# Output weights 6 and 7 and the first projection operand ordered behind the last attention blocks

## The chip, the cores and the metric

The kernel runs on one core of a Trainium2 chip. The metric is the device time of one execution in microseconds (us); lower is better. A core has five engines with a queue each: TensorE (PE, matrix products; PEld is its weight load), VectorE (DVE), ScalarE (ACT), GpSimd (POOL) and SyncE (SP, which here only issues transfers). Each engine takes its instructions in the order that was fixed when the program was built, and an instruction that waits holds up everything behind it on its engine.

## What is computed

The reference is an encoder of two layers on 1024 tokens of width 1024, in float32:

```python
for i in range(2):
    mix = mla_mixer(h, ...) if i == 0 else diff_mixer(h, ...)
    h = layernorm(ALPHA * h + mix)
    h = layernorm(ALPHA * h + swiglu(h))
```

The change lies in layer 0, where the mixer ends and its output projection begins. The mixer is an attention of 8 heads; a token sees the keys of its own chunk of 64 tokens and of all chunks before. With `o` the eight heads' results side by side (8 x 128 = 1024 columns), the mixer returns `o @ w_o`, and the layer goes on with `layernorm(ALPHA * x + o @ w_o)`.

## The kernel before, in words

**Precision by parts.** Products run on a float32 form that TensorE reads in one pass but that keeps fewer bits. So an operand is split in two: ACT casts it to that form (`hi`), and DVE or POOL subtracts (`lo = x - hi`). A product is then three matmuls, hi x hi, hi x lo and lo x hi (`mm3`, L140).

**Attention of layer 0.** Work goes by (head, block of 128 queries). For each block `score_a` (L1141) and `softmax_block` (L206) make the scores on PE (L216), add the mask and find the maximum on DVE (L219), take the exponential on ACT (L222) and the reciprocal of its sum on DVE (L224), and scale the row by it on POOL (L1150). Then `transpose_block` (L227) transposes the block's probabilities on PE (L148), and for each pair of transposed squares ACT makes the hi part `pth` (L243) and DVE the lo part `ptl` (L244). For each pair of blocks, `pv_group` (L246) multiplies with the values on PE (L255), ACT copies the result to `ob` (L1160), and SP stores it to the scratch `o_dr` in memory (L1161). `attention` (L258) runs the blocks of a head in rising order, but those of the last head, 7, in `LAST_ORDER` = 6, 7, 4, 5, 2, 3, 0, 1. Scores run two blocks ahead. The last block of all is therefore block 1 of head 7.

**Output projection.** `out_proj` (L278) loads the eight heads' output weights (128 x 1024 each) and splits them: `load_w` (L128) issues the load on SP (L132), casts on ACT (L136) and subtracts on POOL (L137). Weight 6 goes to a tile of its own pool, and weight 7 to one of the kernel's large tiles; both raw copies lie in the tag `wr`, which has two buffers and is also used by the first loads of the feed-forward part (`gp`, L541). Then, for the token blocks 6, 7, 4, 5, ..., it loads the block's `o` of all heads (`of`, L299; it needs `o_dr` written for head 7), casts it on ACT (`oh`, L302), subtracts on DVE (L303; the profile shows that tile as `oh_a` too), and multiplies: 24 matmuls for each half of the output's columns (three for each head, heads in rising order), into `zp`. DVE adds the residual (L314), and a layer norm follows. The trace calls the first halves' matmuls `zp_a` on L143 to L145.

**What sets the order.** The code is traced as written, and a planner then fixes each engine's order from priorities and from its own model of how long things take. It may put a cast of `out_proj` ahead of attention work that stands earlier in the text, if its model has the cast ready first. `behind(i, j)` (L155) adds an order without a semaphore between two instructions of one engine: `i` stands behind `j` in that engine's queue.

Of the kernel before, what the change touches and what calls it, by code (L numbers as in the profile page):

```python
# [9 lines left out]
F32 = mybir.dt.float32  # L10
F32R = mybir.dt.float32r
AF = mybir.ActivationFunctionType
ALU = mybir.AluOpType
# [3 lines left out]
P = 128  # L17
# [4 lines left out]
H = 8  # L22
# [16 lines left out]
LAST_ORDER = (6, 7, 4, 5, 2, 3, 0, 1)  # L39
# [3 lines left out]
def trunk(  # L43
# [32 lines left out]
    nc = tc.nc  # L76
    V, A, G, T = nc.vector, nc.scalar, nc.gpsimd, nc.tensor
# [9 lines left out]
    wp = ctx.enter_context(tc.tile_pool(name="wp", bufs=3))  # L87
# [19 lines left out]
    def f32(t):  # L107
        return t.bitcast(F32)

    def big_tile(name, dt=F32R):  # L110
        return big.tile([P, 2, 1024], dt, tag="big", name=name)

    def ps_s(name):
        return ps.tile([P, 512], F32, tag="s", bufs=ps_bufs[0], name=name)
# [4 lines left out]
    def ps_t(name):  # L119
        return ps.tile([P, 512], F32, tag="t", bufs=ps_bufs[2], name=name)  # L120
# [4 lines left out]
    def small(name, n=1):  # L125
        return sp.tile([P, 2], F32, tag="small", name=name, bufs=22)[:, :n]

    def load_w(src, cols, name, hi=None, lo=None, eng=None, raw=None, ins=False):  # L128

        if raw is None:  # L130
            raw = wp.tile([P, 1024], F32, tag="wr", bufs=2, name=f"r_{name}")
        nc.sync.dma_start(raw[:, :cols], src)  # L132
        if hi is None:
            hi = wp.tile([P, 1024], F32R, tag="wh", name=f"h_{name}")
            lo = wp.tile([P, 1024], F32R, tag="wl", name=f"l_{name}")
        A.copy(hi[:, :cols], raw[:, :cols])  # L136
        j = (eng or G).tensor_tensor(lo[:, :cols], raw[:, :cols], f32(hi[:, :cols]), ALU.subtract)  # L137
        return (hi, j.ins) if ins else (hi, lo)

    def mm3(ps_out, pairs):  # L140
        n = len(pairs)
        for i, (lh, ll, rh, rl) in enumerate(pairs):
            T.matmul(ps_out, lh, rh, start=(i == 0), stop=False)  # L143
            T.matmul(ps_out, lh, rl, start=False, stop=False)  # L144
            T.matmul(ps_out, ll, rh, start=False, stop=(i == n - 1))  # L145

    def tr(ps_out, in_):
        T.transpose(ps_out, in_, ident)  # L148

    def bcast_row(pool, src, n, name, tag):  # L150
        t = pool.tile([P, n], F32, tag=tag, name=name, bufs=1)
        nc.gpsimd.dma_start(t, src.partition_broadcast(P))
        return t

    def behind(i, j):  # L155

        tc.add_manual_dep(
            i, j.name,
            mybir.DependencyInfo(mybir.DependencyClass.NoSync, mybir.DependencyReason.DATA),
            reason="kept in program order",  # L160
        )
# [37 lines left out]
    def new_xT(pool, name):  # L199
# [3 lines left out]
        }  # L203
        return [[t[p, hf] for hf in range(2)] for p in range(2)]

    def softmax_block(lp, q_pass, s_bias, i, scale, name):  # L206
        n = (i + 1) * P
        nb = 1 if n <= 512 else 2
        w = n // nb
        l = lp.tile([P, 1024], F32, tag="l", name=f"l_{name}")  # L210
        mx = BIGF
        for b in range(nb):
            s = ps_s(f"s_{name}_{b}")
            ks = slice(b * w, (b + 1) * w)
            for j, (lh, rh) in enumerate(q_pass):
                T.matmul(s[:, :w], lh, rh[:, ks], start=(j == 0), stop=(j == len(q_pass) - 1))  # L216
            bv = s_bias[:, 896 - P * i + b * w:896 - P * i + (b + 1) * w]
            m = small(f"mx_{name}_{b}")
            V.tensor_tensor_reduce(l[:, ks], s[:, :w], bv, -scale, mx, ALU.add, ALU.min, m)  # L219
            mx = m  # L220
        sm = small(f"sm_{name}")
        A.activation(l[:, :n], l[:, :n], AF.Exp, bias=mx, scale=-1.0, accum_out=sm)  # L222
        r = small(f"r_{name}")
        V.reciprocal(r, sm)  # L224
        return l, r

    def transpose_block(ptp, pts, l, i, name):  # L227
        qc = (i % 2) * P
        for jq in range(i // 4 + 1):
            nj = min(4, i + 1 - 4 * jq)  # L230
            pt = ps_t(f"pt_{name}_{jq}")
            for jj in range(nj):
                j = 4 * jq + jj
                tr(pt[:, jj * P:(jj + 1) * P], l[:, j * P:(j + 1) * P])
            for jp in range(2 * jq, 2 * jq + (nj + 1) // 2):
                n = min(2, i + 1 - 2 * jp)
                if i % 2 == 0:
                    pts[jp] = tuple(
                        ptp.tile([P, 2, 256], F32R, tag=f"pt{c}", name=f"pt{c}_{name}_{jp}") for c in "hl"
                    )  # L240
                src = pt[:, (jp % 2) * 256:(jp % 2) * 256 + n * P].rearrange("p (j q) -> p j q", j=n)
                hv, lv = (t[:, :n, qc:qc + P] for t in pts[jp])
                A.copy(hv, src)  # L243
                V.tensor_tensor(lv, src, f32(hv), ALU.subtract)  # L244

    def pv_group(pts, g, v_of, name):  # L246
        po = ps_o(f"o_{name}")
# [30 lines left out]
    def out_proj(side, w_o, o_dram, x_src, x_dst, lng, lnb, xo):  # L278


        with tc.tile_pool(name="op0", bufs=2, side=side, reuse_waits="tile") as pool:
            g = bcast_row(pool, lng, D, "mg0", "g")
            b = bcast_row(pool, lnb, D, "mb0", "b")
            wo = []
            for h in range(H):
                dst = ()
                if h in (0, 1, 2, 3, 7):
                    t = big_tile(f"wo0_{h}")
                    dst = (t[:, 0], t[:, 1])
                elif h == 6:  # L290
                    t = pool.tile([P, 2, D], F32R, tag=f"wo{h}", name=f"wo0_{h}", bufs=1)
                    dst = (t[:, 0], t[:, 1])
                wo.append(load_w(w_o[h], 1024, f"wo0_{h}", *dst))
            prev = None
            for tb in LAST_ORDER:
                nm = f"a0_{tb}"
                of = pool.tile([P, H, P], F32, tag="of", name=f"of_{nm}", bufs=2)
                src = o_dram[tb // 2][:, :, (tb % 2) * P:(tb % 2) * P + P]
                nc.sync.dma_start(of, src.rearrange("h p q -> p h q"))  # L299
                ot = pool.tile([P, 2, D], F32R, tag="oh", name=f"oh_{nm}").rearrange("p a (h q) -> p a h q", h=H)  # L300
                oh, ol = ot[:, 0], ot[:, 1]
                A.copy(oh, of)  # L302
                V.tensor_tensor(ol, of, f32(oh), ALU.subtract)  # L303
                zy = pool.tile([P, 2, D], F32, tag="zy", name=f"zy_{nm}")
                z, y = zy[:, 0], zy[:, 1]
                nc.sync.dma_start(z, x_src[tb * P:(tb + 1) * P, :])
                sums = small(f"sum_{nm}", 2)
                junk = []
                for nh in range(2):
                    c = slice(nh * 512, nh * 512 + 512)  # L310
                    m = (ps_m if nh == 0 else ps_t)(f"zp_{nm}_{nh}")
                    junk.append(m)
                    mm3(m, [(oh[:, h, :], ol[:, h, :], wo[h][0][:, c], wo[h][1][:, c]) for h in range(H)])
                    V.scalar_tensor_tensor(  # L314
                        z[:, c], z[:, c], ALPHA, m, ALU.mult, ALU.add, accum_out=sums[:, nh:nh + 1]
                    )
                if tb == LAST_ORDER[-1]:
                    y = big_tile(f"y_{nm}", F32)[:, 0]
                layer_norm(z, sums, junk, y, g, b, nm, x_dst[tb * P:(tb + 1) * P, :])
                if prev is not None:  # L320
                    raw_x(prev[1], xo, prev[0], f"a0_{prev[0]}")
                prev = (tb, y)
        return lambda: raw_x(prev[1], xo, prev[0], f"a0_{prev[0]}")
# [743 lines left out]
    with ast as st:  # L1067
# [73 lines left out]
        def score_a(h, i):  # L1141
            hf, c = i // 4, slice((i % 4) * P, (i % 4) * P + P)
            (qh, ql), (kh, kl), qq = qn[h, hf], kn[h], qr[h, hf]
            l, r = softmax_block(
                lp,
                [(qh[:, c], kh), (qh[:, c], kl), (ql[:, c], kh), (qq[:, c], kr1), (qq[:, c], kr2)],
                ba, i, MLA_SCALE, f"a{h}_{i}",
            )
            n = (i + 1) * P
            G.tensor_scalar(l[:, :n], l[:, :n], r, 1.0, ALU.mult, ALU.mult)  # L1150
            lt[h, i] = l

        def turn_a(h, i):
# [70 lines left out]
    with ExitStack() as st:  # L1224
# [11 lines left out]
        for ql in q_lo:  # L1236
            for mp in range(2):
                b = slice(64 - mp * 64, 128 - mp * 64)
                z = bb[b, :512]
                i = G.tensor_tensor(ql[b, mp * 512:mp * 512 + 512], z, z, ALU.subtract).ins  # L1240
# [147 lines left out]
        first, second = LAST_ORDER[:2]  # L1388
# [110 lines left out]
```

## Time and profile before

| | before |
|---|---|
| time, median of 3 runs | 2296.66 us (2295.4 to 2297.1) |
| the profiled execution | 2296.31 us |
| its span, first to last instruction | 2294.4 us |
| around the span | 1.9 us |
| mean granted TensorE clock | 0.995 |
| PE busy | 2249.9 us, 98% of the span |
| DVE, ACT, POOL busy | 68%, 44%, 38% |

The change touches the stretch from about 340 to 362 us of the span. Times in the views are us from the start of the span. A row of the timeline gives start, duration, engine, line, operation, what it writes and reads, its shape and how many were merged; in square brackets stands how long the engine was idle just before, and what ended that. A row of the table by stages gives the stretch and its length, then the busy time of PE, PEld, DVE, ACT and POOL (with counts), the granted TensorE clock, the share of the DMA engines and GB/s. A merged row carries the shape of its first instruction.

### The profile page before, as it was taken

The numbers are of one execution on the slowest core, as the hardware profiler recorded it, in microseconds if no ns is written. First come the engines' busy times: TensorE is split into PE (matmuls) and PEld (weight loads), VectorE is DVE, ScalarE is ACT, GpSimd is POOL, SyncE is SP. The second block draws the span as 40 slices with busy tenths as digits, with TensorE's granted clock in tenths as the row PEclk, the third lists the DMA queues.
The fourth block names the chain that finished last, engine by engine and source line by source line (L and its number), as shares of the span: only waits on it lengthen the run. The fifth ranks groups of instructions, "written<-read, shape, count | busy, mean of one in ns | idle before, by whom it ended". The sixth has DMA issues, their size and how long they took to land.

```text
span 2294.4 us, 31183 instructions
## 1 busy us (share of the span) xinstructions
PE 2249.9 (98%) x11410; PEld 1915.7 (83%) x11410; DVE 1562.8 (68%) x2899; ACT 1017.9 (44%) x2096; POOL 864.8 (38%) x688
## 2 busy tenths in 40 slices
PE   8999999999999999999999999999999999999997
PEld 8899997878888887888888888987778888887886
DVE  5667664696666668667476667676677666658777
ACT  4455573342333334445465656555432233324353
POOL 2232241114444445555432424221014444436564
PEclk9999999999999999999999999999999999999999
DMA  5010125334435338454310212054244232337353
GB/s 201 14 34 31 41 72 181 136 130 145 177 132 198 125 114 326 184 188 156 102 47 24 66 37 70 19 211 144 96 170 154 72 125 82 130 123 304 141 205 121
DMA packets 105545, 288.28 MB, mean 126 GB/s; under 512 B 7968, under 2 KB 30112, under 8 KB 94896
## 3 DMA queue, kind: packets, MB, share of 16 engines
q1 hardware_dynamic: 100976, 275.87, 33.6%
q0 software_dynamic: 4416, 10.42, 1.6%
q8 instruction: 90, 1.47, 0.3%
q14 instruction: 63, 0.52, 0.1%
HBM read 205.00 MB, written 77.07 MB: 123 GB/s over the span
## 4 chain that ended last, share of the span: by engine, by line
PE 88%; DVE 6%; DMA 3%; issue 2%; ACT 1%; POOL 1%; SPq 0%; DVEq 0%; POOLq 0%; ACTq 0%
PE gb L526 14%; PE gc L526 10%; PE ga L526 10%; PE dw L795 6%; PE zp_a L394 4%; PE s_a L216 4%; PE s_b L216 3%; PE dx L795 3%; PE dv L795 3%; PE bp L143 3%; PE bp L144 3%; PE bp L145 3%; PE dy L795 3%; PE o_a L255 2%; PE o_b L255 2%
## 5 line engine op out<-in xcount | busy, mean ns | idle before, releaser
L480 ACT CAST op_g<-gr 128x512 fp32r<-128x512 f32 x240 | 146.9, 621 | 370.8 <-PE gb L526 183.3
L481 POOL TENSOR_TENSOR op_g<-gr,op_g 128x512 fp32r<-128x512 f32 x104 | 146.4, 1413 | 248.2 <-ACT op_g L480 142.7
L481 DVE TENSOR_TENSOR op_h<-rh,op_h 128x512 fp32r<-128x512 f32 x154 | 163.8, 1091 | 63.4 <-ACT op_h L480 63.4
L526 PE MATMUL ga<-xh_m,op_g 128*128 128x512 f32 x512 | 168.1, 389 | 0.0
L480 ACT CAST op_h<-rh 128x512 fp32r<-128x512 f32 x154 | 92.9, 619 | 136.6 <-PE dx L795 36.1
L795 PE MATMUL dw<-op_w_t,op_h 128*128 128x512 f32 x660 | 151.4, 390 | 0.1
L795 PEld LDWEIGHTS dw<-op_w_t,op_h 128*128 128x128 f32 x660 | 123.6, 188 | 26.0 <-DVE op_h L481 0.5
L222 ACT ACTIVATE l_b<-l_b,mx_b 128x256 f32<-128x256 f32 (+7 forms) x128 | 99.5, 778 | 79.7 <-DVE mx_b L219 77.6
L1303 POOL TENSOR_SCALAR l_b<-l_b,r_b,cst 128x128 f32<-128x128 f32 (+3 forms) x64 | 52.8, 825 | 204.6 <-DVE r_b L224 194.0
L795 PE MATMUL dx<-op_w_b,op_h 128*128 128x512 f32 x528 | 122.2, 391 | 6.8 <-ACT op_w_b L480 3.9
L481 POOL TENSOR_TENSOR op_w_t<-tt,op_w_t 128x512 fp32r<-128x512 f32 x66 | 98.6, 1497 | 79.6 <-ACT op_w_t L480 77.8
L795 PEld LDWEIGHTS dx<-op_w_b,op_h 128*128 128x128 f32 x528 | 98.6, 188 | 30.1 <-ACT op_w_b L480 4.7
L481 DVE TENSOR_TENSOR op_g<-gr,op_g 128x512 fp32r<-128x512 f32 x136 | 110.8, 819 | 15.6 <-ACT op_g L480 15.3
L526 PE MATMUL gb<-t4h_f,op_g 128*128 128x512 f32 x352 | 115.9, 390 | 3.4 <-DVE tmp L609 3.4
L481 POOL TENSOR_TENSOR op_g<-s,op_g 128x512 fp32r<-128x512 f32 x40 | 54.3, 1358 | 167.9 <-ACT op_g L480 159.6
L526 PE MATMUL gb<-t2h_f,op_g 128*128 128x512 f32 x352 | 115.6, 390 | 0.4 <-DVE op_g L481 0.4
L526 PE MATMUL gc<-t1h_f,op_g 128*128 128x512 f32 x352 | 115.4, 389 | 0.0
L526 PE MATMUL gc<-b22h_f,op_g 128*128 128x512 f32 x352 | 115.3, 389 | 0.0
L526 PE MATMUL gb<-t3h_f,op_g 128*128 128x512 f32 x352 | 115.2, 389 | 0.0
L526 PEld LDWEIGHTS ga<-xh_m,op_g 128*128 128x128 f32 x512 | 96.1, 188 | 19.9
L143 PE MATMUL bp<-xT_f,h_wb 128*128 128x512 f32 x256 | 103.0, 402 | 0.0
L145 PE MATMUL bp<-xT_f,l_wb 128*128 128x512 f32 x256 | 101.6, 397 | 0.0
(378 smaller groups left out, 6753.9 us busy)
## 6 DMA issues: line engine op xcount, KB each, us to landing
gr<-in_w_gu SPq DMA_DIRECT2D x44, 1024.0 KB, 6.9
rh<-h_dr SPq DMA_DIRECT2D x28, 1024.0 KB, 4.8
h_dr<-sh SPq DMA_DIRECT2D x22, 1024.0 KB, 5.1
h_dr<-hp SPq DMA_DIRECT2D x22, 768.0 KB, 4.1
tt<-in_w_dn SPq DMA_DIRECT2D x22, 512.0 KB, 7.9
rh<-h_dr SPq DMA_DIRECT2D x14, 768.0 KB, 4.3
wo_dr<-op_pwo SPq DMA_DIRECT2D x16, 512.0 KB, 3.4
z<-xs_dr SPq DMA_DIRECT2D x16, 512.0 KB, 10.0
```

Of the source, the lines that this page charges most:

```text
L143: T.matmul(ps_out, lh, rh, start=(i == 0), stop=False)
L144: T.matmul(ps_out, lh, rl, start=False, stop=False)
L145: T.matmul(ps_out, ll, rh, start=False, stop=(i == n - 1))
L216: T.matmul(s[:, :w], lh, rh[:, ks], start=(j == 0), stop=(j == len(q_pass) - 1))
L222: A.activation(l[:, :n], l[:, :n], AF.Exp, bias=mx, scale=-1.0, accum_out=sm)
L255: T.matmul(po[:, c], a, b[:, j % 2, c], start=st, stop=sp_, skip_group_check=True)
L394: T.matmul(m, a[:, h, :], self.wo[h][w][:, c], start=(start and h == heads[0] and a is oh and w == 0), stop=(stop and h == heads[-1] and a ...
L480: A.copy(hi, src)
L481: return eng.tensor_tensor(lo, src, f32(hi), ALU.subtract).ins
L526: T.matmul(o, w[:, a, kc], x[b][:, k, :], start=(first and k == 0 and (a, b) == (0, 0)), stop=(k == 3 and a == 1), skip_group_check=True,)
L795: T.matmul(o, h[:, a, c], w[:, b_], start=(first and (a, b_) == (0, 0)), stop=(last and a == 1), skip_group_check=True,)
L1303: G.tensor_scalar(l1[:, :n], l1[:, :n], r1, nlam, ALU.mult, ALU.mult)
```

## The change

It does five things. `ends` remembers the last exponential (ACT), the last scaling (POOL, L1150) and the last `pth` and `ptl` that were traced, which are those of head 7's block 1. Weight 6 is still cast on ACT and subtracted on POOL, but behind the last exponential and behind the last scaling. The first token block's `oh` and `ol` (block 6) are made in two halves of four heads, on the same engines as before, behind the last `pth` and the last `ptl`. Weight 7 is cast on ACT behind the second half of `oh`, and its subtraction goes from POOL to DVE, behind the second half of `ol`. The loads of both raw weights stay where they were in the text. Nothing else is changed, and the result is computed by the same operations.

```diff
+    ends = {}
+
     def softmax_block(lp, q_pass, s_bias, i, scale, name):
...
-        A.activation(l[:, :n], l[:, :n], AF.Exp, bias=mx, scale=-1.0, accum_out=sm)
+        ends["exp"] = A.activation(l[:, :n], l[:, :n], AF.Exp, bias=mx, scale=-1.0, accum_out=sm).ins
...
-                A.copy(hv, src)
-                V.tensor_tensor(lv, src, f32(hv), ALU.subtract)
+                ends["pth"] = A.copy(hv, src).ins
+                ends["ptl"] = V.tensor_tensor(lv, src, f32(hv), ALU.subtract).ins
...
-                wo.append(load_w(w_o[h], 1024, f"wo0_{h}", *dst))
+                if h < H - 2:
+                    wo.append(load_w(w_o[h], 1024, f"wo0_{h}", *dst))
+                    continue
+                raw = wp.tile([P, 1024], F32, tag="wr", bufs=2, name=f"r_wo0_{h}")
+                nc.sync.dma_start(raw, w_o[h])
+                wo.append(dst)
+                if h == H - 2:
+                    behind(A.copy(dst[0], raw).ins, ends["exp"])
+                    behind(G.tensor_tensor(dst[1], raw, f32(dst[0]), ALU.subtract).ins, ends["norm"])
...
-                A.copy(oh, of)
-                V.tensor_tensor(ol, of, f32(oh), ALU.subtract)
+                first = tb == LAST_ORDER[0]
+                for hs in (slice(0, 4), slice(4, 8)) if first else (slice(0, 8),):
+                    i = A.copy(oh[:, hs], of[:, hs]).ins
+                    j = V.tensor_tensor(ol[:, hs], of[:, hs], f32(oh[:, hs]), ALU.subtract).ins
+                    if first:
+                        behind(i, ends["pth"])
+                        behind(j, ends["ptl"])
+                if first:
+                    behind(A.copy(wo[-1][0], raw).ins, i)
+                    behind(V.tensor_tensor(wo[-1][1], raw, f32(wo[-1][0]), ALU.subtract).ins, j)
...
-            G.tensor_scalar(l[:, :n], l[:, :n], r, 1.0, ALU.mult, ALU.mult)
+            ends["norm"] = G.tensor_scalar(l[:, :n], l[:, :n], r, 1.0, ALU.mult, ALU.mult).ins
```

## The prediction

> **What bounds the kernel now.** I read the page first, then the table by stages around the change, then each engine's timeline there, and last a table over the whole span in stretches of 3.41 us.
>
> ```profile
> PE 2249.9 (98%) x11410; PEld 1915.7 (83%) x11410; DVE 1562.8 (68%) x2899; ACT 1017.9 (44%) x2096; POOL 864.8 (38%) x688
> PE 88%; DVE 6%; DMA 3%; issue 2%; ACT 1%; POOL 1%; SPq 0%; DVEq 0%; POOLq 0%; ACTq 0%
> ```
>
> PE is busy for 98% of the span and 88% of the chain that ended last, so time can come only from holes in PE or from stretches in which it runs slowly. The stage of the change has both.
>
> ```profile
> 345.00:350.00 5.00, 3.11 (x21) 2.38 (x20) 2.37 (x5) 3.33 (x9) 4.94 (x3) 1.00 1.02 371
> 350.00:357.00 7.00, 5.96 (x19) 4.99 (x20) 3.12 (x5) 2.33 (x5) 0.00 (x0) 0.51 1.02 351
> ```
>
> PE is idle for 1.9 of the five us from 345, and for the next seven its granted clock is 0.51. Its own timeline:
>
> ```profile
> 347.30 0.28 PE L255 MATMUL o_a<-pth_a,vl 128*128 128x256 f32 x1
> 349.17 0.39 PE L255 MATMUL o_a<-pth_a,vh 128*128 128x256 f32 x1 [1.60 <-ACT pth_a L243]
> 350.24 0.58 PE L255 MATMUL o_a<-pth_a,vh 128*128 128x256 f32 x1 [0.46 <-ACT pth_a L243]
> 351.62 0.58 PE L255 MATMUL o_a<-ptl_a,vh 128*128 128x256 f32 x1 [0.80 <-DVE ptl_a L244]
> 353.81 0.73 PE L143 MATMUL zp_a<-wo,oh_a 128*128 128x512 f32 x1
> 360.81 0.39 PE L143 MATMUL zp_a<-wo,oh_a 128*128 128x512 f32 x1
> ```
>
> Three waits (2.86 us) lie ahead of the projection, whose first matmul comes at 353.81 and whose second column half comes at 360.81, 24 matmuls and 7.00 us later. ACT and DVE show why:
>
> ```profile
> 342.92 1.05 ACT L136 CAST wo<-r_wo 128x1024 fp32r<-128x1024 f32 x1
> 343.86 0.65 ACT L243 CAST pth_a<-pt_a 128x256 fp32r<-128x256 f32 x2
> 344.39 0.53 ACT L222 ACTIVATE l_a<-l_a,mx_a 128x256 f32<-128x256 f32 x1
> 344.80 0.21 ACT L222 ACTIVATION_READ_ACCUMULATOR l_a<-l_a,mx_a 128x1 f32 x1
> 344.89 1.05 ACT L136 CAST wo<-r_wo 128x1024 fp32r<-128x1024 f32 x1
> 345.83 0.55 ACT L243 CAST pth_a<-pt_a 128x256 fp32r<-128x256 f32 x2
> 347.36 1.04 ACT L302 CAST oh_a<-of_a 128x1024 fp32r<-128x1024 f32 x1 [0.98 <-DMA of_a<-o_dr]
> 348.58 0.54 ACT L243 CAST pth_a<-pt_a 128x128 fp32r<-128x128 f32 x2
> 349.81 0.37 ACT L243 CAST pth_a<-pt_a 128x256 fp32r<-128x256 f32 x1 [0.69 <-PE pt_a L148]
> 353.79 1.04 ACT L302 CAST oh_a<-of_a 128x1024 fp32r<-128x1024 f32 x1 [0.43 <-DMA of_a<-o_dr]
> ```
>
> ```profile
> 348.44 2.59 DVE L303 TENSOR_TENSOR oh_a<-of_a,oh_a 128x1024 fp32r<-128x1024 f32 x1 [1.57 <-ACT oh_a L302]
> 350.95 0.94 DVE L244 TENSOR_TENSOR ptl_a<-pt_a,pth_a 128x128 fp32r<-128x128 f32 x3
> 354.87 1.23 DVE L303 TENSOR_TENSOR oh_a<-of_a,oh_a 128x1024 fp32r<-128x1024 f32 x1 [2.97 <-ACT oh_a L302]
> ```
>
> On ACT the cast of the first `oh` stands ahead of the last three `pth`: it waits 0.98 us for its load and takes 1.04. On DVE its subtraction stands ahead of the last three `ptl` and takes 2.59 us, where the next one takes 1.23. Two weight casts of 1.05 us sit ahead of other `pth` and of the last exponential (344.39). POOL:
>
> ```profile
> 344.77 2.40 POOL L137 TENSOR_TENSOR wo<-r_wo,wo 128x1024 fp32r<-128x1024 f32 x1
> 347.15 0.47 POOL L1150 TENSOR_SCALAR l_a<-l_a,r_a 128x256 f32<-128x256 f32 x1
> 347.60 2.34 POOL L137 TENSOR_TENSOR wo<-r_wo,wo 128x1024 fp32r<-128x1024 f32 x1
> ```
>
> The scaling of the very last block stands behind a weight's subtraction of 2.40 us. So each of three queues does projection work first that PE needs later.
>
> **Part by part.** *Scaling of the last block.* Its row sum is out at 345.01 (344.80 + 0.21). POOL was free at 344.77, where the weight's subtraction began. Without that it starts once the reciprocal is there, about 345.2, or sooner if the exponential moves up by the 1.05 us cast: 1.9 us or more earlier than 347.15.
>
> *The last `pth` and `ptl`.* The one weight cast left early may again follow the exponential and cost its 1.05 us there; the other is gone. Without the wait for `oh`, the last `pth` follow their transposes. PE itself then sets the pace. From 351.62 ten matmuls take 2.40 us at half clock (this chain row stands below), so 0.12 us each at full clock; twelve of them and two transposes remain after 347.42 in the timeline above, about 1.6 us. They would end at 349.0 if nothing ahead of 347.30 moved. The cast gone at 342.92 lets the matmuls ahead of those start some 0.4 to 0.7 us sooner, less what the last `ptl` chain still holds up. I take 348.6 as the end of attention on PE (before: 353.8).
>
> ```profile
> 343.33 4.01 DMA of_a<-o_dr
> ...
> 351.62 2.40 PE o_a L255 x10
> ```
>
> ```profile
> L480 ACT CAST op_g<-gr 128x512 fp32r<-128x512 f32 x240 | 146.9, 621 | 370.8 <-PE gb L526 183.3
> ```
>
> *First operand.* Its load is issued at 343.33 and has landed after 4.01 us, at 347.34 (the chain; the cast's own shape stands in the page's row). Nothing in the change moves the attention result that it waits for, so that stays. A half of `oh` is a 128 x 512 cast, 0.62 us by the row of that shape. The floor for the projection is thus 347.34 + 0.62 = 348.0. Behind the last `pth` (about 347.6) the halves run to 348.2 and 348.8; half of 1.23 is 0.62 us for each half of `ol`, ready at 348.8 and 349.4. The third matmul (349.05) needs the first, the fifteenth (351.8) the second: the two extra instructions hide behind PE. Start: 348.6, bounds 348.0 and 349.0.
>
> *Weights 6 and 7.* Heads 6 and 7 are needed from the 19th and 22nd matmul. How long 24 take at full clock:
>
> ```profile
> 361.01 0.69 DVE L314 SCALAR_TENSOR_TENSOR zy_a<-zy_a,zp_a 128x512 f32<-128x512 f32 x1 [4.92 <-PE zp_a L145]
> 366.45 0.69 DVE L314 SCALAR_TENSOR_TENSOR zy_a<-zy_a,zp_a 128x512 f32<-128x512 f32 x1 [4.74 <-PE zp_a L145]
> ```
>
> DVE waits for the two column halves of one block 5.44 us apart, 0.227 us a matmul. So weight 6 is due at 352.7 and weight 7's lo at 353.6. Weight 6: POOL from about 345.7 for 2.40 us, 348.1. Weight 7: ACT 348.8 to 349.85, DVE 1.23 us, 351.1. They are early by 4.6 and 2.5 us, hidden behind the earlier heads' matmuls; without that cover PE would wait for the remainder one to one. Behind weight 7 on ACT stand the copies of the last attention results and the cast of the second block's `oh`; the latter's load lands at 353.79 in any case, and it is due at 354.0 + 5.4 = 359.4.
>
> *DVE against POOL.* The subtraction from 348.44 overlaps POOL's from 347.60 and ends 1.09 us after it (351.03 against 349.94), as if it had started only then; the `ptl`, which read PSUM and one tile, took no longer. If POOL's weight 6 began just ahead of `ol`, the third matmul would wait to 348.1 + 2.40 + 0.62 = 351.1, a stall of 2.1 us; by the order above POOL is done at 348.1, and I take none. The Trainium skill, "SBUF — State Buffer", section "SBUF: two separate sides", says that DVE with two SBUF inputs and a reading GpSimd op hold the shared port pair in turns, each for a whole instruction; this trace agrees with 2.59 against 1.23 us, and by that rule weight 7's move to DVE risks at most one such hold.
>
> *Clock.* Rows of the table in 3.41 us stretches:
>
> ```profile
> 346.67:350.08 3.41, 1.45 (x8) 1.01 (x8) 1.84 (x3) 2.02 (x5) 3.27 (x3) 1.00 1.02 404
> 350.08:353.50 3.42, 2.46 (x10) 2.17 (x11) 1.81 (x4) 0.48 (x2) 0.00 (x0) 0.50 1.02 309
> 503.68:507.10 3.42, 2.02 (x10) 1.33 (x9) 3.39 (x6) 1.14 (x2) 0.33 (x1) 1.00 0.00 0
> 507.10:510.51 3.41, 3.41 (x17) 2.82 (x16) 3.41 (x6) 0.62 (x1) 0.00 (x0) 1.00 0.41 148
> 1643.74:1647.15 3.41, 1.32 (x8) 0.82 (x8) 2.97 (x5) 1.59 (x3) 0.93 (x1) 1.00 0.82 271
> 1647.15:1650.56 3.41, 3.41 (x13) 2.92 (x11) 1.51 (x3) 1.66 (x4) 0.00 (x0) 0.50 0.98 383
> ```
>
> After stretches with PE busy for 1.45 and 1.32 us the next ran at 0.50; after one with 2.02 us it did not. The change leaves at most 1 us of holes, 2.4 us busy, so I take full clock throughout. That is worth 7.00 - 5.44 = 1.56 us on the first 24 matmuls.
>
> *SP's queue.* Weight 7's raw buffer is now freed by DVE at about 351.1.
>
> ```profile
> 353.38 0.32 SPq L1161 DMA_DIRECT2D o_dr<-ob  x1
> 353.75 0.42 SPq L541 DMA_DIRECT2D gp<-in_w_gu  x1
> ```
>
> The load that takes over that buffer (353.75) stood behind a store at 353.38 anyway, so that wait costs nothing.
>
> *Sum.* The second column half starts at 348.6 + 5.44 = 354.0 where it started at 360.8: 6.8 us less. From there on PE has no large hole in this stage, and everything later follows PE, so I carry all of it to the end. The profiled execution took 2296.3 (span 2294.4 and 1.9 around it); 2289.5 comes out. The median lies 0.35 above that execution: 2289.9. With the bounds of the start the gain is 7.4 to 6.4, with the port held 4.7.
>
> **Rivals.** *A, the clock stays half for a stretch, or POOL holds the port.* Holes of over 1.5 us in one stretch would do it, since 1.45 us busy did. One halved stretch gives back half of 3.41, 1.7 us, two 3.4, the port 2.1: gains of 5.1 to 3.4, times 2291.5 to 2293.3. For it: POOL is late if the planner puts weight 6's cast late on ACT. Against: the holes left are 1 us at most. Chance 0.18. It could also be that the half clock of before had another cause than the holes and stays: the 1.56 us are not won, 2291.4; against that stands that the stretches above with as little work were followed by half clock too. Chance 0.04. The Trainium skill, "TensorE: Matmul & The Clock Gate", section "Why this matters for your kernels", puts the idle gap that drops the clock at over about 3 us, which would make this last case the true one; the trace disagrees, with half clock after a largest hole of 1.60 us.
>
> *B, nothing comes of it.* `behind` orders only what it names. If the planner lets the two casts of the first feed-forward load (their raw buffer is weight 6's) into ACT ahead of weight 7, ACT waits for a landing there:
>
> ```profile
> 356.65 1.14 ACT L480 CAST op_gp<-gp 128x512 fp32r<-128x512 f32 x2 [0.81 <-DMA gp<-in_w_gu]
> ```
>
> Weight 7 would then be cast at 357.8 and subtracted by 360.1, and the two matmuls left of the first half end at 360.6, where they end now: no gain, 2296 to 2297. Chance 0.10.
>
> *C, slower: the same two casts ahead of the first half of `oh`.* Then `oh` is ready at 357.8 + 0.6 = 358.4, PE has been idle for ten us, and the first stretch runs at half clock: 5.44 + 1.7 us, second half at 365.5, 4.7 us later than now: 2301.4. It decides as soon as the wait sits there and the load lands after 351. For it: in the run of before ACT's order did put a cast that waits for a load ahead of work that was ready (347.36). Against: those casts stand after the whole projection in the text, and came behind two `oh` there. Chance 0.08.
>
> **How the numbers follow.** Forecast 0.60, A 0.22, B 0.10, C 0.08; the likeliest gives 2289.9. About 0.2% (4.6 us) is what a measurement of this kernel can tell from no change. The forecast is faster; of A half is (0.11, a single halved stretch) and the rest within; B is within; C slower: 0.71, 0.21, 0.08. The range keeps the forecast and A and leaves out B and C, 0.18: up to 2294.5; down to 2287.5, for a start at 348.0 (7.4 us) and one of the later halved stretches (1.7 us) going away as stages shift.
>
> **What would show it.** Right: ACT shows the last `pth` ahead of both halves of `oh`, DVE the last `ptl` ahead of `ol`, POOL the last scaling near 345, no half clock from 350 to 357, the first `zp_a` near 348.6 and its second half near 354. Wrong: a wait of `zp_a` for weight 7 or for `ol`, a wait for a `gp` load on ACT ahead of them, a clock of 0.5 there, or a stage that ends 7 us earlier while a later one ends no earlier.

## The result, and the profile after

| | before | after |
|---|---|---|
| time, median | 2295.34 us (2293.3 to 2297.9, 8 runs) | 2289.38 us (2287.0 to 2290.4, 8 runs) |
| ratio after to before | | 0.9972, 95% interval 0.9963 to 0.9981 |
| profiled execution: time, span | 2296.3, 2294.4 us | 2287.0, 2284.9 us |

The change makes the kernel faster by 6.0 us, or 0.28%. The five runs of before that came in with the result put its median 1.3 us below the one shown first. The two profiled executions differ by 9.3 us, more than the medians do; where the rest lies is told below. Lines from L206 on have moved down by up to 19 in the new kernel.

The page after, its first line:

```profile
PE 2244.2 (98%) x11410; PEld 1910.8 (84%) x11410; DVE 1561.1 (68%) x2901; ACT 1017.7 (45%) x2097; POOL 861.2 (38%) x687
```

PE's busy time fell by 5.7 us with as many matmuls as before, and the mean granted clock of the profiled execution rose from 0.995 to 0.997. The table by stages of the new kernel (stretch and length; busy PE, PEld, DVE, ACT, POOL; clock; DMA share; GB/s):

```profile
343.50:347.00 3.50, 3.43 (x28) 3.18 (x27) 2.12 (x6) 2.55 (x8) 2.51 (x2) 1.00 1.02 350
347.00:350.50 3.50, 3.50 (x16) 2.66 (x16) 2.16 (x3) 1.34 (x3) 0.00 (x0) 1.00 0.87 307
350.50:357.00 6.50, 6.50 (x30) 5.39 (x29) 1.83 (x3) 2.56 (x4) 1.04 (x1) 1.00 1.00 364
```

The holes are gone and the clock stays at 1.00. To compare executions that began differently, I read the stage from one fixed event on PE, the four transposes of head 7's block 5, to the first matmul of the projection's second column half. In the timeline of before the first is

```profile
340.98 0.62 PE L148 MATMUL pt_a<-ident,l_a 128*128 128x128 f32 x4
```

and the last stands in the prediction at 360.81, so the stage took 19.83 us. After:

```profile
339.38 0.62 PE L148 MATMUL pt_a<-ident,l_a 128*128 128x128 f32 x4
...
346.71 0.27 PE L258 MATMUL o_a<-pth_a,vl 128*128 128x128 f32 x1
346.82 0.45 PE L143 MATMUL zp_a<-wo,oh_a 128*128 128x512 f32 x1
347.11 0.40 PE L144 MATMUL zp_a<-wo,oh_a 128*128 128x512 f32 x1
347.38 0.50 PE L145 MATMUL zp_a<-wo,oh_a 128*128 128x512 f32 x1
...
352.49 0.39 PE L143 MATMUL zp_a<-wo,oh_a 128*128 128x512 f32 x1
```

It takes 13.11 us, 6.72 less. PE goes from the last attention matmul (346.71) into the projection (346.82) with no hole. This execution is 1.60 us early where the stage begins (339.38 against 340.98); add that to compare its times with those of the prediction. The queues that feed PE, ACT, DVE and POOL in turn:

```profile
344.40 0.55 ACT L246 CAST pth_a<-pt_a 128x128 fp32r<-128x128 f32 x2
345.30 0.37 ACT L246 CAST pth_a<-pt_a 128x256 fp32r<-128x256 f32 x1 [0.36 <-PE pt_a L148]
345.99 1.14 ACT L315 CAST oh_a<-of_a 128x512 fp32r<-128x512 f32 x2 [0.31 <-DMA of_a<-o_dr]
347.03 1.05 ACT L321 CAST wo<-r_wo 128x1024 fp32r<-128x1024 f32 x1
```

```profile
345.71 0.42 DVE L247 TENSOR_TENSOR ptl_a<-pt_a,pth_a 128x256 fp32r<-128x256 f32 x1 [0.30 <-ACT pth_a L246]
346.63 1.29 DVE L316 TENSOR_TENSOR oh_a<-of_a,oh_a 128x512 fp32r<-128x512 f32 x2 [0.50 <-ACT oh_a L315]
348.11 1.23 DVE L322 TENSOR_TENSOR wo<-r_wo,wo 128x1024 fp32r<-128x1024 f32 x1 [0.18 <-ACT wo L321]
```

```profile
343.19 0.49 POOL L1169 TENSOR_SCALAR l_a<-l_a,r_a 128x256 f32<-128x256 f32 x1
343.64 2.37 POOL L304 TENSOR_TENSOR wo<-r_wo,wo 128x1024 fp32r<-128x1024 f32 x1
```

The last `pth` now stand ahead of the operand on ACT, the last `ptl` ahead of it on DVE, and POOL scales the last block at 343.19 (344.79 on the old scale, where it was 347.15). Weight 6 is subtracted from 343.64 to 346.01, so POOL is out of the way when DVE begins the operand at 346.63: its two halves take 1.29 us together, where the whole took 2.59 before. The operand's load lands just before 345.99 (347.59 on the old scale) and is no longer waited for by work that PE needs sooner.

### The profile page after: what moved, and what is told of

Its sections match the earlier page's. It is cut to its first block, busy times and chain, and to the rows that moved or that the text cites. A ratio compares the mean times of both kernels' runs of the same rounds, so it can differ in the third digit from the quotient of the medians.

```text
span 2284.9 us, 31183 instructions
## 1 busy us (share of the span) xinstructions
PE 2244.2 (98%) x11410; PEld 1910.8 (84%) x11410; DVE 1561.1 (68%) x2901; ACT 1017.7 (45%) x2097; POOL 861.2 (38%) x687
## 4 chain that ended last, share of the span: by engine, by line
PE 87%; DVE 5%; DMA 3%; ACT 2%; issue 1%; POOL 1%; SPq 0%; DVEq 0%; POOLq 0%; ACTq 0%
PE gb L545 14%; PE gc L545 10%; PE ga L545 8%; PE dw L814 7%; PE s_a L219 4%; PE zp_a L413 4%; PE dx L814 3%; PE s_b L219 3%; PE dv L814 3%; PE dy L814 3%; PE bp L143 3%; PE bp L144 3%; PE bp L145 3%; PE o_a L258 2%; PE o_b L258 2%; PE hq L1019 1%
```

## The experiments

Theory 1: the cost lay in the order on ACT and DVE, where the first operand stood ahead of the last `pth` and `ptl`; the late scaling behind weight 7's subtraction is the smaller part. Its rival: the weights are the main part. Theory 2, on the clock: it halves after a stretch of 3.41 us in which PE was busy for less than about half, whatever the longest gap. Its rivals: only a gap of over 3 us does it, or something else does, such as the transfers. Stages were read as above, in the profiled execution of each kernel.

| kernel | stage, us | against before | first 24 matmuls, us | time, median | ratio to before (95%) |
|---|---|---|---|---|---|
| before | 19.83 | | 7.00 | 2295.34 | |
| the change | 13.11 | -6.72 | 5.67 | 2289.38 | 0.9972 (0.9963 to 0.9981) |
| operand alone | 14.78 | -5.05 | 5.53 | 2289.46 | 0.9971 (0.9960 to 0.9982) |
| weights alone | 18.01 | -1.82 | 6.85 | 2294.16 | 0.9993 (0.9983 to 1.0002) |
| operand in one piece | 13.79 | -6.04 | 6.37 | 2288.11 | 0.9971 (0.9960 to 0.9982) |
| weight 7 on POOL | 12.98 | -6.85 | 5.55 | 2287.74 | 0.9966 (0.9953 to 0.9979) |
| a hole | 17.10 | -2.73 | 7.00 | 2293.22 (one run) | |
| the hole filled | 15.98 | -3.85 | 5.74 | 2294.84 (one run) | |

For the four kernels in the middle the ratio is to runs of before beside them, 2295.4 us in the median. The whole times do not tell the change, the operand alone, the operand in one piece and weight 7 on POOL apart, as their intervals overlap; they tell these four from before, and the weights alone not.

**The operand alone.** Weights 6 and 7 are made as all others are, where they are loaded. Against the change:

```diff
-                if h < H - 2:
...
-                    behind(A.copy(dst[0], raw).ins, ends["exp"])
-                    behind(G.tensor_tensor(dst[1], raw, f32(dst[0]), ALU.subtract).ins, ends["norm"])
+                wo.append(load_w(w_o[h], 1024, f"wo0_{h}", *dst))
...
-                if first:
-                    behind(A.copy(wo[-1][0], raw).ins, i)
-                    behind(V.tensor_tensor(wo[-1][1], raw, f32(wo[-1][0]), ALU.subtract).ins, j)
```

> Only the first operand's two halves stand behind the last pth and ptl; weights 6 and 7 are cast and subtracted as before. I read the stage from the transposes of head 7's block 5 on PE (340.98 before) to the first matmul of the second column half (360.81 before): 19.83 us before, 13.11 after the change. Theory 1 (the operand ahead of the last pth and ptl was the main cost): the last scaling on POOL stays late behind weight 7's subtraction, the last pth comes some 1.2 us later than after the change, and the first ol half waits about 0.9 us for POOL's weight 6; the stage takes about 14.6 us, 5.2 less than before, and the whole time lies near 2290.5. Rival (the weight casts and the late scaling were the main cost): the stage takes 17 us or more.

Its PE, its POOL, and last its ACT and DVE:

```profile
340.43 0.62 PE L148 MATMUL pt_a<-ident,l_a 128*128 128x128 f32 x4
...
355.21 0.39 PE L143 MATMUL zp_a<-wo,oh_a 128*128 128x512 f32 x1
```

```profile
344.22 2.41 POOL L137 TENSOR_TENSOR wo<-r_wo,wo 128x1024 fp32r<-128x1024 f32 x1
346.59 0.48 POOL L1158 TENSOR_SCALAR l_a<-l_a,r_a 128x256 f32<-128x256 f32 x1
```

```profile
348.16 0.38 ACT L246 CAST pth_a<-pt_a 128x256 fp32r<-128x256 f32 x1
...
349.09 1.48 DVE L308 TENSOR_TENSOR oh_a<-of_a,oh_a 128x512 fp32r<-128x512 f32 x2
```

14.78 us, as theory 1 had it; three quarters of the gain come with this part. How much of it is ACT's order and how much DVE's was not taken apart. The scaling is as late as before (346.59, behind 2.41 us of weight 7), and the last `pth` (348.16) comes 1.8 us later after the start of the stage than with the change, and the projection with it. The 0.9 us for POOL's port, a term of that expectation, came out as 0.2: POOL's second subtraction (347.04, 2.37 us) ended 0.32 us after the first `ol` half began, the two halves took 1.48 us where the change needs 1.29, and PE did not wait for them.

**The weights alone.** Against the change:

```diff
-                for hs in (slice(0, 4), slice(4, 8)) if first else (slice(0, 8),):
+                for hs in (slice(0, 8),):
...
-                    if first:
-                        behind(i, ends["pth"])
-                        behind(j, ends["ptl"])
```

> Only the weights are moved: weight 6 behind the last exponential and scaling, weight 7 behind the whole operand on ACT and DVE; the operand is cast in one piece and free to go ahead of the last pth and ptl. Theory 1: the last pth waits on ACT for the operand and weight 7, the last ptl on DVE for both subtractions; PE idles for about 4 us, the clock drops to half, and the stage takes about 18 us, 1.8 less than before; whole time near 2293.5, hard to tell from no change. Rival (weights were the main cost): 15 us or less, near 2290.

```profile
340.28 0.62 PE L148 MATMUL pt_a<-ident,l_a 128*128 128x128 f32 x4
...
349.00 0.38 PE L258 MATMUL o_a<-pth_a,vh 128*128 128x256 f32 x1 [1.85 <-ACT pth_a L246]
350.51 0.39 PE L258 MATMUL o_a<-ptl_a,vh 128*128 128x256 f32 x1 [1.13 <-DVE ptl_a L247]
...
358.29 0.39 PE L143 MATMUL zp_a<-wo,oh_a 128*128 128x512 f32 x1
```

```profile
347.36:350.78 3.42, 0.65 (x3) 0.46 (x4) 2.70 (x3) 1.86 (x4) 0.00 (x0) 1.00 1.01 322
350.78:354.19 3.41, 3.41 (x12) 2.83 (x12) 0.00 (x0) 0.79 (x1) 0.00 (x0) 0.50 1.06 382
```

18.01 us: the waits for the last `pth` and `ptl` (1.85 and 1.13 us) are back, because operand and weight 7 stand ahead of them, and with PE busy for 0.65 us in one stretch the next runs at half clock. The two waits make 2.98 us, where about 4 were expected; the stage came out as forecast. The whole time cannot be told from before. So the rival of theory 1 falls. The two parts nearly add up: 5.05 + 1.82 = 6.87, against 6.72. The clock's share of the gain lies wholly in the first part: the kernel with the operand alone runs this stage at full clock, the one with the weights alone does not.

**The operand in one piece.** The first line of the diff just above, alone.

> The change with the first operand in one piece behind the last pth and ptl. Theory 1: the first matmul comes 0.4 us later (a cast of 1.04 in place of 0.62), the third waits for the whole subtraction, 0.8 us in all: the stage takes 13.9 us against 13.1, the whole time is 0.8 us above the change, within its scatter. Rival (halving brings nothing, PE is still in attention then): 13.1 us. A second rival (halving is what lets PE go on): over 15 us, with half clock.

```profile
339.71 0.62 PE L148 MATMUL pt_a<-ident,l_a 128*128 128x128 f32 x4
...
348.38 0.50 PE L145 MATMUL zp_a<-wo,oh_a 128*128 128x512 f32 x1 [0.53 <-DVE oh_a L316]
...
353.50 0.39 PE L143 MATMUL zp_a<-wo,oh_a 128*128 128x512 f32 x1
```

13.79 us: halving is worth 0.68 us, and it is the third matmul that waits, for the whole subtraction. The first one came no later than with the change (7.42 us after the start of the stage, against 7.44), though 0.4 us had been expected for the longer cast: PE was still in attention then.

**Weight 7 on POOL.**

```diff
-                    behind(V.tensor_tensor(wo[-1][1], raw, f32(wo[-1][0]), ALU.subtract).ins, j)
+                    behind(G.tensor_tensor(wo[-1][1], raw, f32(wo[-1][0]), ALU.subtract).ins, ends["norm"])
```

> The change with weight 7's subtraction on POOL behind weight 6's, no longer on DVE. Theory 1: it runs from about 348.1 to 350.4 in the time of the changed profile, and head 7 is due at 351.8: the stage keeps its 13.1 us, the whole time that of the change. Rival (the move to DVE carries part of the gain, since POOL is late or holds the port while DVE subtracts): 14 us or more, with a wait of zp for weight 7.

```profile
340.16 0.62 PE L148 MATMUL pt_a<-ident,l_a 128*128 128x128 f32 x4
...
353.14 0.39 PE L143 MATMUL zp_a<-wo,oh_a 128*128 128x512 f32 x1
```

12.98 us; the subtraction starts on POOL at 348.68 and takes 2.39 us, so head 7's lo is ready at 351.07, and its matmul comes later. The move to DVE brings nothing here. What weight 6 and weight 7 are worth each was not taken apart. No kernel here beats the change by more than the runs can tell.

**A hole, and the same hole filled.** Weight 7's cast is made three times, all ahead of the operand and behind the last `pth`, and not again behind the operand. Against the change:

```diff
+                if first:
+                    again = [A.copy(wo[-1][0], raw).ins for _ in range(3)]
+                    behind(again[0], ends["pth"])
...
+                    ends["pth"] = again[-1]
...
-                    behind(A.copy(wo[-1][0], raw).ins, i)
```

The second kernel has twelve spare matmuls besides, chained behind the last attention matmul (`ends["pv"]`, which it keeps for this); their result is not used:

```diff
+                    spare = ps_s("spare")
+                    last = ends["pv"]
+                    for k in range(12):
+                        m = T.matmul(spare, wo[0][0][:, :P], wo[0][0][:, :512], start=(k == 0), stop=(k == 11)).ins
+                        behind(m, last)
+                        last = m
```

> The change with weight 7's cast made three times over, all ahead of the operand's halves on ACT: the operand comes about 2.95 us later and PE has one hole of about that length just ahead of the projection. Theory 2 (the clock halves after a 3.41 us stretch in which PE was busy for less than some 1.5 to 2 us, whatever the longest gap): with most of the hole in one stretch, which is more likely than not, the next stretch runs at 0.50; the stage takes 13.1 + 2.95 + 1.7 = 17.8 us. If the hole is split evenly over two stretches, or if it takes a gap of more than 3 us, the clock stays full and the stage takes 16.1 us.

> The same delay, and twelve spare matmuls of 128 x 512 (2.7 us, their product is not used) on PE between the last attention matmul and the projection. Theory 2: PE is busy in the hole, so the clock stays at full in every case, and the stage takes 16.1 us with the operand as late as in the kernel with the open hole. Rival (the half clock comes from something else, such as the transfers that run at the same time): half clock as with the open hole.

The kernel with the hole, its PE and two rows of its table by stages (its clock changes at 351.04):

```profile
341.27 0.62 PE L148 MATMUL pt_a<-ident,l_a 128*128 128x128 f32 x4
...
351.37 0.79 PE L143 MATMUL zp_a<-wo,oh_a 128*128 128x512 f32 x1 [2.51 <-ACT oh_a L321]
...
358.37 0.39 PE L143 MATMUL zp_a<-wo,oh_a 128*128 128x512 f32 x1
```

```profile
347.63:351.04 3.41, 1.23 (x11) 1.09 (x10) 0.39 (x1) 3.38 (x5) 0.28 (x1) 1.00 0.89 350
351.04:354.45 3.41, 3.08 (x7) 2.44 (x8) 2.43 (x3) 1.16 (x3) 0.00 (x0) 0.50 0.97 335
```

And the kernel with the hole filled:

```profile
340.25 0.62 PE L148 MATMUL pt_a<-ident,l_a 128*128 128x128 f32 x4
...
347.67 2.98 PE L323 MATMUL spare<-wo 128*128 128x512 f32 x12
350.49 0.39 PE L143 MATMUL zp_a<-wo,oh_a 128*128 128x512 f32 x1
...
356.23 0.39 PE L143 MATMUL zp_a<-wo,oh_a 128*128 128x512 f32 x1
```

```profile
348.40:351.81 3.41, 3.41 (x15) 2.46 (x14) 1.47 (x3) 2.40 (x4) 0.00 (x0) 1.00 0.99 294
351.81:355.23 3.42, 3.42 (x17) 2.79 (x16) 2.14 (x2) 1.42 (x2) 0.00 (x0) 1.00 0.99 387
```

A hole of 2.51 us halved the clock for one stretch, and the first 24 matmuls took 7.00 us; with PE kept busy through the same delay, and transfers as dense (DMA share near 1 in both), the clock stayed full and they took 5.74. The rows of the filled kernel are stretches of its own clock, found by counting back from a later change of it at 870.64 in steps of 3.4133 us (before, 213 such steps lie between the changes at 1558.40 and 2285.44). In the first of them the spare matmuls stand for about 2.1 us, from 348.40 to 350.49. Without them PE would have had 1.3 us of work there, no more than where the clock was halved; so it was the filling that kept it full. So neither a gap of over 3 us nor the transfers by themselves are what halves the clock, and both rivals fall.

The expected 17.8 us came out as 17.10. The hole was 0.3 us shorter than the extra casts, and the half clock cost 1.3 us and not 1.7: the halved stretch began 0.33 us ahead of the first matmul, which is worth half of that, and the 0.2 us of waits that the change has among its first 24 matmuls did not come on top (7.00 is 5.44 and half of the 3.08 us that PE ran halved). Two single runs say nothing on the whole time here: the filled kernel has the shorter stage and the longer run. Against before, it lost 3.7 us near 1088, where PE has a hole of 3.02 us and half clock behind it that no other of these profiles has; why it is there stays open. The planner also ordered a few later instructions of it differently.

## Why the prediction was right

- *The last scaling*, forecast for 345.2 or sooner: 344.79 on the old scale. Right. In the kernel with the operand alone it stays late, and the stage is 1.67 us longer, with both weights' casts in their old places as well.
- *End of attention and start of the projection*, forecast 348.6 with bounds 348.0 and 349.0: 348.42 (346.82 + 1.60). PE's own matmuls set it, as the step said.
- *First operand.* ACT's halves came at the time that was forecast, 347.59 against about 347.6, but not for its reason: they waited 0.31 us for the load, which landed 0.2 us later than the 347.34 of before, and not for the last `pth`. The first matmul did not wait for them. That the subtraction hides behind PE was nearly right: the third matmul follows the second by 0.27 instead of 0.23 us and is itself lengthened; 5.67 us for the 24 instead of 5.44 is that 0.2 us. Making the operand whole turns it into a wait of 0.53.
- *Weights 6 and 7*, forecast ready 4.6 and 2.5 us early: weight 7's lo ends at 349.34 and its first matmul, the 23rd, comes at 352.0. Right, with 2.7 us to spare. That its engine does not matter is what this step implied, and the run on POOL shows it.
- *DVE against POOL.* The change does not meet the hold, as assumed: POOL is done at 346.01, DVE begins at 346.63. The Trainium skill, "SBUF — State Buffer", section "SBUF: two separate sides", describes the hold; the whole operand took 2.59 us before under POOL's 2.34 us, and 1.23 us in the kernel with the operand in one piece, where POOL was idle by then.
- *Clock*, 1.56 us: full in the stage after. Rival A put the holes that it takes at over 1.5 us in one stretch, which is too low: 1.45 us of work leaves 1.96 us of holes, and after, a stretch with 1.88 us of work, 1.53 of holes, was followed by full clock. Its cause, holes that fall into one stretch, is real: it cost the kernel with the weights alone 1.4 us (6.85 against 5.44 for 24 matmuls) and the one with the hole 1.3 (7.00 against 5.74 with the hole filled). The Trainium skill, "TensorE: Matmul & The Clock Gate", section "Why this matters for your kernels", puts the gap at over about 3 us; here one of 2.51 us halved the clock, and the measurement decides.
- *SP's queue.* The second early load is issued earlier than before, as the wait it inherits ends with weight 7; PE kept its lead of 8.3 us up to 860 us of the span, so nothing it needed came late.
- *Rivals B and C* did not come: the feed-forward's first casts stayed behind the second operand on ACT.
- *Sum*: 6.8 us forecast in the stage, 6.72 measured. All of it was carried on: matched matmul by matmul, the new execution is 1.60 us ahead of the old one from about 34 us of the span up to the stage, 8.32 just behind it, and 9.4 at the end of PE's work. So the stage explains 6.72 of the 9.3 us between the two profiles; 1.6 were there before the change acts, and 1.1 came later, as the net of gains and losses, some of them told below. The medians, 6.0 us apart, contain both kinds of scatter; their interval, a gain of 4.4 to 8.5 us, cannot confirm the 6.8 any more closely. That the forecast time, 2289.9, lies only 0.5 us from the measured median is in part luck: before itself came out 1.3 us lower than the runs that the forecast started from, and the gain 0.8 us smaller.

## What to carry to other kernels

At a seam between two stages, look at each in-order queue for work of the next stage that waits for a load, or takes long, ahead of the last short pieces that TensorE still needs from the old one; an order without a semaphore puts it right. Why the planner had put it there was not looked at. Price such a hole with the clock that it may cost behind it, not by its length alone. Read a small gain in the stage, between two fixed events on the bounding engine, since here the whole times scatter by nearly as much as the change is worth.

## What the runs showed of the hardware that I had not expected

The 3.41 us stretches begin at other places in each execution, and with them moves the place where the same holes cost clock. Before, at a later seam that the change doesn't touch:

```profile
1554.99:1558.40 3.41, 1.49 (x11) 1.24 (x11) 2.63 (x10) 2.30 (x7) 1.60 (x3) 1.00 0.81 286
1558.40:1561.81 3.41, 3.41 (x9) 2.41 (x8) 2.87 (x3) 2.57 (x8) 2.36 (x2) 0.50 0.09 12
```

After, on that execution's own stretches, at the same seam, at the one after it (halved before, in the prediction's last rows of the clock), and at one that was not halved before:

```profile
1545.14:1548.56 3.42, 1.97 (x16) 1.77 (x14) 3.01 (x13) 1.75 (x7) 1.25 (x2) 1.00 1.00 339
1548.56:1551.97 3.41, 1.88 (x9) 1.27 (x9) 1.83 (x7) 2.76 (x7) 2.06 (x2) 1.00 0.25 101
...
1633.89:1637.30 3.41, 1.75 (x8) 1.13 (x6) 2.97 (x5) 1.57 (x3) 0.93 (x1) 1.00 0.86 270
1637.30:1640.72 3.42, 2.99 (x17) 2.63 (x18) 1.99 (x4) 1.00 (x3) 0.00 (x0) 1.00 1.03 382
...
862.48:865.89 3.41, 1.46 (x7) 0.92 (x6) 2.59 (x5) 1.25 (x3) 0.23 (x1) 1.00 1.01 405
865.89:869.30 3.41, 3.41 (x10) 2.63 (x9) 3.38 (x3) 1.65 (x3) 3.25 (x3) 0.50 0.98 294
```

From 20 us of the span on, and in all eight kernels, every stretch at full clock with 1.50 us of work or less was followed by half clock, and every one with 1.67 or more was not. Between them lie three, and there the busy time of the profile does not decide. Two stand in the kernel with the hole, each with the stretch behind it:

```profile
1504.75:1508.16 3.41, 1.63 (x6) 0.74 (x6) 3.38 (x7) 0.56 (x3) 0.56 (x1) 1.00 1.03 419
1508.16:1511.57 3.41, 3.41 (x13) 2.96 (x13) 1.95 (x9) 2.04 (x5) 0.00 (x0) 0.50 1.00 417
...
2061.12:2064.53 3.41, 1.51 (x7) 0.94 (x5) 2.59 (x5) 1.15 (x4) 0.00 (x0) 1.00 0.02 10
2064.53:2067.95 3.42, 3.36 (x15) 2.75 (x16) 3.38 (x4) 1.79 (x5) 3.04 (x2) 1.00 0.67 214
```

1.63 us of work with a longest gap of 1.28 us was followed by half clock, 1.51 us with a gap of 1.95 us was not, and neither were 1.58 us in the kernel after (from 2057.14). So the bound lies near 44% to 49% busy, the longest gap is not what decides, and the busy time is only close to it; what exactly counts stays open. Transfers were dense in the first of the three (DMA share 1.03) and few in the others (0.02 and 0.14), so a part of theirs within this narrow band is not excluded. At the seam above, the hole that fell into one stretch before was split over two after, with 1.97 and 1.88 us of work, and cost no clock. Nor does a halved stretch end the matter by itself: before, the stretch that ran at half clock from 350.08 had 2.46 us of work, and the next was halved too. What it takes to come back to full was not tried. Two seams halved before and not after, one after and not before: differences of this kind can be part of the scatter of a us or two between runs. They do not explain all that arose behind the stage. At the seam near 1647 the lead of the new execution grew from 9.0 to 10.6 us, and by 1673 it was 8.9 again; the 1.1 us are what was left of several such gains and losses.
